# Attention's probabilities transposed by VectorE and through DRAM, the values scaled in place of them, and retention's output products among the filling

## The chip, the cores and the metric

One core of one Trainium2 chip runs the whole block. The metric is the device time in microseconds (us); lower is better. The kernel before takes 691.04 us, the median of three runs (690.86 to 691.95). Its engines are named as in the profile: PE is TensorE (matmuls, and transposes done as matmuls), PEld its weight loads, DVE is VectorE, ACT ScalarE, POOL GpSimd and SP SyncE, which issues nearly all DMA transfers. PSUM is the memory that matmuls write, in banks of 128 partitions x 512 float32; tiles are 128 partitions high.

## What is computed

A decoder block on 512 tokens of 1024 features, all in float32: retention (4 heads) and forgetting attention (8 heads of 64) beside each other, mixed by sigmoid gates, then an output product and a SwiGLU. The change touches the attention, the two output products and the gates. Cut to these:

```python
z = rmsnorm(x, g_mix) @ w_in              # q_r,k_r,v_r,g_r, q_f,k_f,v_f,f_f, a_r,a_f
o_r = silu(g_r) * groupnorm(retention(rotary(q_r), rotary(k_r), v_r))
y_r = o_r @ w_ret_o                        # 512 -> 1024
# forgetting attention, per head; c is the running sum of log sigmoid(f_f + b)
s = (q @ k.T) / 8 + c[:, None] - c[None, :]
s = where(key <= query, s, -inf)
p = softmax(s, axis=-1)                    # exp(s - max) divided by its row's sum
o_f = p @ v
y_f = o_f @ w_fox_o                        # 512 -> 1024
merged = sigmoid(a_r) * y_r + sigmoid(a_f) * y_f
x = x + merged @ w_out
x = x + swiglu(rmsnorm(x))
```

## The kernel before

Most products are made of three matmuls (`three`, L171): each float32 operand is split into a part that the fast matmul format holds exactly (`wh`, `xh`, cast by ScalarE in line 153 for weights) and the rest (`wl`, `xl`, subtracted by VectorE in line 154). A unit of weights is a tile `raw` of 128 x 1024 (512 KB), loaded by SyncE in line 146; each `split_w` (L157) splits the unit that was loaded ahead and asks for a later one.

TensorE's order is pinned: `in_order` (L65) ties every matmul to the one before it. The other engines' orders come from a scheduler, with a few ties made by `after`. The program walks through its stages with `fill(us)` between the steps: `Fill` (L283) is a queue of generators of independent matmuls, the filling, and takes that many microseconds' worth from its head; `fill.until(n)` empties it until n generators are left. The filling is the projections of queries, keys and values, then the gates' projections: `gates(mp)` (L755) makes two gates (g = 0 for retention, 1 for attention) of two feature tiles each, 48 matmuls of 512 columns for each g, whose results VectorE takes from PSUM times `r1` into `sg` (L759).

The attention is the loop of lines 847 to 862, a chain of 32 steps s: a pair of heads a (0 to 3), a head e of the pair, a query tile i from 3 down to 0, with (i + 1) x 128 keys that are not masked. A step has these parts:

- `fox_scores` (L692): two matmuls into a bank `sc` (two banks, `sc`); VectorE's `tensor_tensor_reduce` (L710) subtracts the scores from the bias tile `cb` and keeps the row minimum; ScalarE's exponential (L712) makes the probabilities `pr` and their row sums; VectorE takes the reciprocal (L713) and multiplies `pr` by it (L714).
- `fox_turn` (L717), three steps later (`LAG`): i + 1 transposes of 128 x 128 on TensorE (through `turn`, L75) into a bank `tp`, copied into the head's `pT` by VectorE for i = 3 (L727) and by ScalarE for the other tiles (L729): 80 transposes and 32 copies in all.
- `fox_values` (L731), once a pair: 8 float32 matmuls of `vf` by `pT` into one bank `sc`, split into `ofh` (ScalarE, L177) and `ofl` (VectorE, L178).
- `fox_prep` (L673), in four of a pair's eight steps: the scaled queries `tq` and keys `tk` with their low parts (VectorE, L689); of the keys, a DMA copies the half `tk` to the other partitions (L687). `fox_bias` (L645) fetches `cb`, a head's row spread over 128 partitions (L648, 256 KB).

Between the steps stand 0.63 to 1.57 us of filling (`SF`), before a pair's values 1.8 (`VF`). Lines 870 to 887 come next: for each pair of feature tiles the output products of retention (from `orh`, `orl`) and of attention (from `ofh`, `ofl`), 24 matmuls each, the sigmoids on ScalarE and four operations of VectorE for each tile. With the pinning off there, the scheduler places some of retention's products beside the attention's last steps. `merged @ w_out` follows (L939), then the SwiGLU.

An operation that the change takes over is already there for the heads of queries and keys: `turn_heads` (L653) transposes all 32 x 32 squares of a tile at once on VectorE (`STREAM_TRANSPOSE`), and `put_heads` (L660) puts the squares to DRAM and fetches them into their places.

## Time and profile before

| what | us |
|---|---|
| median of the three runs | 691.04 |
| the profiled execution, its own time | 690.54 |
| its span in the trace, first to last instruction | 688.5 |
| first score matmul to the start of the first attention output product | 182.93 to 262.26 |
| first values of the four pairs (start) | 204.56, 224.22, 243.63, 256.64 |
| first matmul of `merged @ w_out` | 311.2 |

All times of the trace count from the span's start. A row of the timeline has the start in us, the duration in us, engine, line, operation, result and operands, then in brackets how long the engine had been idle and what released it. Matmuls overlap: one of 512 columns is shown with 0.39 us, and the next one starts 0.23 us after it. A group's row has the busy sum in us and the mean of one in ns behind the first bar, and the idle time ahead of the group behind the second. A stretch's row has its length and then, for TensorE, weight loads, VectorE, ScalarE and GpSimd, the busy time in it with the number of instructions; then the granted clock, the DMA engines' share and GB/s. A row of DMA issues ends with the KB of one and the median us from issue to landing.

### The profile page before, as it was taken

Reading aid. Unit: us, or ns where it says so; the run is one execution under the profiler, and the core shown is the slowest. Engines: PE = TensorE matmul, PEld = TensorE weight load, DVE = VectorE, ACT = ScalarE, POOL = GpSimd, SP = SyncE. Lnnn points to the kernel's source line nnn. Section 1 sums busy time; section 2 is a strip of 40 time slices with the busy share of each in tenths; the row PEclk is TensorE's granted clock in tenths of the full one; section 3 lists DMA queues with packets and bytes.
Section 4 is the critical chain, followed back from the end, with each engine's and each line's share of the span. In section 5 each row is a group of like instructions: output and inputs, shape, how many; then the busy total and the mean of one; then the engine's idle time right before and its main releaser. Section 6 shows DMA issues by size and latency. Waiting matters only on the chain.

```text
span 688.5 us, 9502 instructions
## 1 busy us (share of the span) xinstructions
PE 682.9 (99%) x3487; PEld 572.6 (83%) x3487; DVE 538.0 (78%) x873; ACT 360.3 (52%) x542; POOL 70.2 (10%) x88
## 2 busy tenths in 40 slices
PE   9999999999999999999999999999999999999998
PEld 6888988888878778888888888888888898888997
DVE  6899478766598866647979998989999888557694
ACT  6767362332466666325566655565647475433341
POOL 0004941200132110000130000000000000000000
PEclk9999999999999999999999999999999999999999
DMA  8900314465432412238510615546362541642211
GB/s 285 419 34 32 124 62 137 109 181 136 160 107 78 137 47 78 93 99 298 214 61 1 243 33 144 152 117 180 89 178 60 131 145 32 187 149 66 105 75 62
DMA packets 85326, 86.73 MB, mean 126 GB/s; under 512 B 63000, under 2 KB 63640, under 8 KB 84768
## 3 DMA queue, kind: packets, MB, share of 16 engines
q1 hardware_dynamic: 85136, 86.12, 40.2%
q8 instruction: 27, 0.44, 0.3%
q14 instruction: 19, 0.16, 0.1%
q10 hardware_dynamic: 144, 0.02, 0.0%
HBM read 75.61 MB, written 4.21 MB: 116 GB/s over the span
## 4 chain that ended last, share of the span: by engine, by line
PE 91%; DVE 4%; DMA 2%; ACT 1%; issue 1%; SPq 1%; POOL 0%; ACTq 0%; DVEq 0%; POOLq 0%
PE acc L72 69%; PE sc L72 16%; PE tp L72 5%; PE tp L75 2%; DVE pr L710 1%; DMA raw<-in_w_dn_dram 1%; DMA raw<-in_w_tok_dram 0%; ACT pr L712 0%; DMA cb<-cd 0%; DVE ps L970 0%; DVE wl L154 0%; DVE pT L727 0%; SPq L1074 0%; ACT ps L969 0%; DVE pr L714 0%
## 5 line engine op out<-in xcount | busy, mean ns | idle before, releaser
L72 PE MATMUL acc<-ps,xfh 128*128 128x512 f32 (+1 forms) x576 | 166.6, 372 | 0.3 <-ACT us L1091 0.3
L72 PEld LDWEIGHTS acc<-ps,xfh 128*128 128x128 f32 x576 | 105.2, 188 | 19.2 <-ACT us L1091 0.5
L969 ACT CAST ps<-b 128x1024 fp32r<-128x1024 f32 (+1 forms) x84 | 82.3, 980 | 62.4 <-DVE b L978 27.4
L970 DVE TENSOR_TENSOR ps<-b,ps 128x1024 fp32r<-128x1024 f32 (+1 forms) x84 | 94.3, 1135 | 19.4 <-ACT ps L969 18.3
L72 PE MATMUL acc<-ps,xfl 128*128 128x512 f32 (+1 forms) x288 | 106.9, 371 | 0.0
L153 ACT CAST wh<-raw 128x1024 fp32r<-128x1024 f32 (+1 forms) x44 | 46.0, 1049 | 85.0 <-PE acc L72 60.2
L154 DVE TENSOR_TENSOR wl<-raw,wh 128x1024 fp32r<-128x1024 f32 (+1 forms) x44 | 56.5, 1287 | 18.5 <-ACT wh L153 18.4
L72 PEld LDWEIGHTS acc<-ps,xfl 128*128 128x128 f32 x288 | 54.3, 188 | 9.4
L72 PE MATMUL acc<-xh,wh 128*128 128x512 f32 x128 | 52.9, 413 | 0.0
L978 DVE TENSOR_TENSOR b<-b,b 128x1024 f32<-128x1024 f32 (+1 forms) x48 | 52.2, 1126 | 0.2 <-DMA b<-in_w_gu_dram 0.2
L72 PE MATMUL acc<-wh,xh 128*128 128x512 f32 (+2 forms) x144 | 50.4, 350 | 0.0
L72 PE MATMUL acc<-xh,wl 128*128 128x512 f32 x128 | 50.1, 392 | 0.0
L72 PE MATMUL acc<-xl,wh 128*128 128x512 f32 x128 | 50.0, 391 | 0.0
L72 PE MATMUL acc<-wh,xl 128*128 128x512 f32 (+2 forms) x144 | 49.4, 343 | 0.0
L72 PE MATMUL acc<-wl,xh 128*128 128x512 f32 (+2 forms) x144 | 49.3, 342 | 0.0
L72 PE MATMUL acc<-hl,ps 128*128 128x512 f32 x168 | 40.4, 389 | 0.0
L72 PEld LDWEIGHTS acc<-hl,ps 128*128 128x128 f32 x168 | 31.5, 188 | 6.6
L1091 ACT COPY us<-acc 128x512 f32<-128x512 f32 (+1 forms) x48 | 26.1, 550 | 15.6 <-PE acc L72 14.5
L72 PEld LDWEIGHTS acc<-wh,xh 128*128 128x128 f32 x144 | 27.2, 189 | 3.6 <-ACT wh L153 0.2
L72 PEld LDWEIGHTS acc<-wh,xl 128*128 128x128 f32 x144 | 27.2, 189 | 3.2
L1010 DVE TENSOR_TENSOR ps<-raw,ps 128x1024 fp32r<-128x1024 f32 x14 | 17.1, 1223 | 16.3 <-ACT ps L1007 16.3
L72 PEld LDWEIGHTS acc<-wl,xh 128*128 128x128 f32 x144 | 27.2, 189 | 3.0
(294 smaller groups left out, 1473.1 us busy)
## 6 DMA issues: line engine op xcount, KB each, us to landing
b<-in_w_gu_dram SPq DMA_DIRECT2D x40, 512.0 KB, 4.9
raw<-in_w_a_dram SPq DMA_DIRECT2D x16, 512.0 KB, 3.6
raw<-in_w_dn_dram SPq DMA_DIRECT2D x14, 512.0 KB, 4.8
pf<-squares SPq DMA_DIRECT2D x160, 32.0 KB, 1.9
blk<-in_w_vg_dram SPq DMA_DIRECT2D x8, 512.0 KB, 13.0
raw<-in_w_tok_dram SPq DMA_DIRECT2D x8, 512.0 KB, 3.4
raw<-in_w_y_dram SPq DMA_DIRECT2D x8, 512.0 KB, 3.7
raw<-in_w_o_dram SPq DMA_DIRECT2D x8, 512.0 KB, 3.8
```

Of the source, the lines that this page charges most:

```text
L72: in_order(nc.tensor.matmul(o, **kw))
L75: in_order(nc.tensor.transpose(out=o, in_=src, identity=ident))
L153: split_raw.last = (nc.scalar.copy(out=h[:, :width], in_=raw[:, :width]), tt(out=l[:, :width], in0=raw[:, :width], in1=f32(h)[:, :width], ...
L154: tt(out=l[:, :width], in0=raw[:, :width], in1=f32(h)[:, :width], op=ALU.subtract))
L710: nc.vector.tensor_tensor_reduce(out=pr[:, :n], in0=cb[:, :n], in1=sc[:, :n], scale=-1.0, scalar=3e38, op0=ALU.add, op1=ALU.min, accum_out=nm)
L969: part.cast = nc.scalar.copy(out=h, in_=raw)
L970: low = tt(out=l, in0=raw, in1=f32(h), op=ALU.subtract)
L978: queue(tt(out=raws[g][b][v], in0=raws[g][b][v], in1=raws[g][c][v], op=ALU.add))
L1010: tt(out=l, in0=raw, in1=f32(h), op=ALU.subtract)
L1091: copy = nc.scalar.copy(out=u_(tp, slot), in_=os[tp][:, :w])
```

## The change

The probabilities stay unnormalised: the reciprocal and the multiplication of each step go (L713, L714). The row sums of a pair's eight tiles are collected in `rs`, VectorE takes their reciprocals at once, and the result goes to DRAM (`rd`) and comes back spread over the partitions (`rw`). VectorE multiplies the values by `rw` in PSUM before they are split.

TensorE's transposes and their copies go too. `fox_turn` has VectorE transpose a tile's probabilities within 32 x 32 squares into the head's `psq` (1 or 2 instructions a tile: 32 of 256 elements a partition and 16 of 128 in all); `fox_put` puts `psq` to DRAM (640 KB a head), and `fox_get` fetches it with four DMAs of 160 KB into `pT`, which puts the squares into their places. The values are taken two pairs of steps after their scores began (in steps 16, 24, 32 and 40; the loop has nine trailing steps), and their columns stand by square.

The transfers of SyncE now keep the program's order (`move`), those of weights, bias tiles, keys and probabilities among them; a load of weights is asked for two `three`s after a unit was taken, in place of at once. Scores and values take turns over the four banks `sc` and `tp`. `gates(3)` stands in the filling whole, and behind it retention's four output products, each with its sigmoid and its multiplication; the last stage keeps the attention's output products. There are 16 tiles `sg` for 14, three `cb` for two.

```diff
+    def move(to, src):
+        ins = nc.sync.dma_start(out=to, in_=src)
+        if moves[0]:
+            if moves[1] is not None:
+                after(ins, moves[1])
+            moves[1] = ins
+        return ins
...
-    RAW, WB, SG, PT, CBUF = 2, 3, 14, 2, 2
-    RF, CF, PF, SF, LAG = (5.72, 4.64, 5.6, 4.6, 11.2), (3.0, 2.0, 2.26, 4.0), 5.9, (0.63, 0.83, 1.57, 1.4), 3
-    VF = 1.8
+    RAW, WB, SG, PT, CBUF, LEAD = 2, 3, 16, 2, 3, 2
+    RF, CF, PF, SF, LAG = (5.72, 4.64, 5.6, 4.6, 11.2), (3.0, 2.0, 2.26, 4.0), 5.9, (0.63, 0.83, 1.57, 1.4), 2
+    VF, TAIL = 1.8, 2.6
...
         h = fwk.tile([P, S], F32R, name=("tk", "tq")[part], tag=f"{('tk', 'tq')[part]}{e}", bufs=1)
         act(out=h[r], in_=zr, func=AF.Copy, scale=gr)
-        if part == 0:
-            nc.sync.dma_start(out=f32(h)[o], in_=f32(h)[r])
...
+    def next_bank():
+        fox["banks"] = fox.get("banks", 0) + 1
+        return bank(("sc", "tp")[fox["banks"] % 2])
...
-        sc = bank("sc")
+        sc = next_bank()
         mm(sc[:, :m], lhsT=tq[:, qs], rhs=tk[:, :m], start=True, stop=False)
         mm(sc[:, :m], lhsT=tq[:, qs], rhs=kl[:, :m], start=False, stop=True)
         pr = fwk.tile([P, n], F32, name="pr", tag=f"pr{i}", bufs=1)
         nm = sm.tile([P, 1], F32, name="nm", tag="nm", bufs=4)
-        rs = sm.tile([P, 1], F32, name="rs", tag="rs", bufs=4)
-        ri = sm.tile([P, 1], F32, name="ri", tag="ri", bufs=4)
         nc.vector.tensor_tensor_reduce(out=pr[:, :n], in0=cb[:, :n], in1=sc[:, :n], scale=-1.0, scalar=3e38,
                                        op0=ALU.add, op1=ALU.min, accum_out=nm)
-        fox["last"] = act(out=pr[:, :n], in_=pr[:, :n], func=AF.Exp, scale=-1.0, bias=nm, accum_out=rs)
-        nc.vector.reciprocal(out=ri, in_=rs)
-        ts(out=pr[:, :n], in0=pr[:, :n], scalar1=ri, scalar2=None, op0=ALU.mult)
+        fox["last"] = act(out=pr[:, :n], in_=pr[:, :n], func=AF.Exp, scale=-1.0, bias=nm, accum_out=fox["rs", a][:, e, i:i + 1])
         fox["pr", a, e, i] = pr
     def fox_turn(a, e, i):
-        pr, pT = fox["pr", a, e, i], fox["pT", a, e]
-        pt = bank("tp")
-        for j in range(i + 1):
-            turn(pt[:, j * P:(j + 1) * P], pr[:, j * P:(j + 1) * P])
-        row = pT[:, i * P:(i + 1) * P]
-        dst = bass.AP(tensor=row.tensor, offset=row.offset, ap=[row.ap[0], [384, i + 1], [1, P]])
-        src = pt[:, :(i + 1) * P].rearrange("p (j q) -> p j q", j=i + 1)
-        if i == 3:
-            nc.vector.tensor_copy(out=dst, in_=src)
-        else:
-            nc.scalar.copy(out=dst, in_=src)
+        if i == NT - 1:
+            fox["sq", a, e] = fwk.tile([P, 4, 10, 32], F32, name="psq", tag="psq", bufs=PSQ)
+        pr, to = fox["pr", a, e, i], fox["sq", a, e].rearrange("p b c j -> p c b j")
+        squares_ = pr.rearrange("p (k b j) -> p k b j", b=4, j=32)
+        for k0, k1, step in ((0, min(i, 1), 3), (2, i, 1)):
+            if k1 >= k0:
+                c = TRI[k0] + i
+                nc.vector.transpose(out=to[:, c:c + (k1 - k0) * step + 1:step], in_=squares_[:, k0:k1 + 1])
+    def fox_put(a, e):
+        pd = fox["pd", e] = drp.tile([4, 32, 4, 320], F32, name="pd", tag=f"pd{e}")
+        move(pd.rearrange("g m b x -> (g m) (b x)"), fox["sq", a, e].rearrange("p b c j -> p (b c j)"))
+        if e:
+            ri = sm.tile([P, 2, NT], F32, name="ri", tag="ri", bufs=2)
+            nc.vector.reciprocal(out=ri, in_=fox["rs", a])
+            rd = fox["rd", e] = drp.tile([2, NT, P], F32, name="rd", tag="rd")
+            move(rd.rearrange("e i p -> p e i"), ri)
+    def fox_get(a, e):
+        pT = fox["pT", a, e] = fwk.tile([P, 4, 320], F32, name="pT", tag="pT", bufs=PT)
+        for b in range(4):
+            move(pT[32 * b:32 * b + 32], fox["pd", e][:, :, b, :].rearrange("g m x -> m g x"))
+        if e:
+            rw = fox["rw", a] = fwk.tile([P, S], F32, name="rw", tag="rw", bufs=1)
+            for h, rows in enumerate((ra, rb)):
+                move(rw[rows], fox["rd", e][h:h + 1].rearrange("o i p -> o (i p)").broadcast_to([FD, S]))
     def fox_values(a):
-        av = bank("sc")
-        for j in range(NT):
+        av = next_bank()
+        o = av.rearrange("p (g i j) -> p g i j", g=4, i=NT)
+        for k in range(NT):
+            c = TRI[k] + k
             for e in range(2):
-                mm(av[e * FD:(e + 1) * FD, j * P:], lhsT=vf[:, j, (2 * a + e) * FD:(2 * a + e + 1) * FD],
-                   rhs=fox["pT", a, e][:, j * 512:j * 384 + 512], start=j == 0, stop=j == NT - 1)
-        split_ps(av, ofh[:, a, :], ofl[:, a, :])
+                mm(o[e * FD:(e + 1) * FD, :, k:, :].rearrange("p g i j -> p g (i j)"), lhsT=vf[:, k, (2 * a + e) * FD:(2 * a + e + 1) * FD],
+                   rhs=fox["pT", a, e][:, :, 32 * c:32 * (c + NT - k)], start=k == 0, stop=k == NT - 1)
+        o = o.rearrange("p g i j -> p i g j")
+        first = tt(out=o, in0=o, in1=fox["rw", a].rearrange("p (i g j) -> p i g j", i=NT, g=4), op=ALU.mult)
+        after(first, split_raw.last[1])
+        if a == 3:
+            after(first, y_ret.last)
+        h, l = (f[:, a, :].rearrange("p (i g j) -> p i g j", i=NT, g=4) for f in (ofh, ofl))
+        cast = nc.scalar.copy(out=h, in_=o)
+        after(cast, split_raw.last[0])
+        if a == 3:
+            after(cast, sigmoid.last)
+        tt(out=l, in0=o, in1=f32(h), op=ALU.subtract)
...
+    def y_ret(mp):
+        def evac(m2, acc):
+            s0 = sig[0, 2 * mp + m2]
+            sigmoid(s0)
+            y_ret.last = tt(out=s0, in0=acc, in1=s0, op=ALU.mult)
+        yield from feat(lambda u: w_y[0, mp], 1, orh, orl, evac)
...
-                tok_group(unit(1), evac_kf), tok_group(unit(0), evac_to(vf, AF.Copy)), gates(0), gates(1), gates(2), gates(3, (0,)))
+                tok_group(unit(1), evac_kf), tok_group(unit(0), evac_to(vf, AF.Copy)), gates(0), gates(1), gates(2), gates(3), *(y_ret(mp) for mp in range(4)))
...
     chain = [(a, e, i) for a in range(4) for e in range(2) for i in reversed(range(NT))]
-    for s in range(len(chain) + LAG + 2):
-        if s < len(chain) and s % 8 < 2:
-            fox_prep(s // 8, 1, s % 8)
-        if s % 8 in (4, 5) and s // 8 < 3:
-            fox_prep(s // 8 + 1, 0, s % 8 - 4)
+    for s in range(len(chain) + 9):
+        a, n = s // 8, s % 8
+        if n < 2 and a < 4:
+            fox_prep(a, 1, n)
+        if n in (4, 5) and a < 3:
+            fox_prep(a + 1, 0, n - 4)
         if s < len(chain):
             fox_scores(*chain[s])
-        v = s - LAG - 1
-        if v >= 0 and v % 8 == 7:
-            fill(VF + 2.0 * (v == len(chain) - 1))
-            if v == 7:
-                fill.until(4)
-            fox_values(v // 8)
+        if n == 1 and a < 4:
+            fox_twice(1)
+        if n == 5 and a < 3:
+            fox_twice(0)
+        if n in (1, 5) and 2 * a + n // 4 + 2 < FH:
+            fox["bias"].append(fox_bias(2 * a + n // 4 + 2))
+        if n == 0 and a > 1:
+            fill(VF)
+            if a == 2:
+                fill.until(8)
+            if a == 5:
+                ready.append(split_raw(begun.pop(0)))
+            fox_values(a - 2)
+        if n == 7 and a < 4 or n == 3 and 0 < a < 5:
+            fox_put(*chain[s - 7 + 3][:2])
+        if n in (1, 5) and 0 < a < 5:
+            fox_get(*chain[s - 9 + 3][:2])
         if LAG <= s < len(chain) + LAG:
             fox_turn(*chain[s - LAG])
-        fill(SF[chain[s][2]] if s < len(chain) else SF[0] + 0.8)
-    fill.until(3)
...
+    fill.until(0)
     for mp in range(4):
-        if mp > 0:
-            fill.until(3 - mp)
-            if mp == 3:
-                run(gates(mp, (1,)))
         ys = []
-        for g, (yh, yl) in enumerate(((orh, orl), (ofh, ofl))):
-            run(feat(lambda u: w_y[g, mp], 1, yh, yl, lambda m2, acc: ys.append(acc)))
+        run(feat(lambda u: w_y[1, mp], 1, ofh, ofl, lambda m2, acc: ys.append(acc)))
         for m2 in range(2):
             m = 2 * mp + m2
             s0, s1 = sig[0, m], sig[1, m]
-            for sg in (s0, s1):
-                after(act(out=sg, in_=sg, func=AF.Sigmoid), fox["last"])
-            tt(out=s0, in0=ys[m2], in1=s0, op=ALU.mult)
-            tt(out=s1, in0=ys[2 + m2], in1=s1, op=ALU.mult)
+            sigmoid(s1)
+            tt(out=s1, in0=ys[m2], in1=s1, op=ALU.mult)
```

Of the names below, `acc` tiles are the filling's PSUM banks, `wl` a weight unit's low part, `sg` a gate, `pr` a tile of probabilities, `nm` its row minimum; line numbers are those of the kernel that the rows are from.

VectorE before, just ahead of the first score step (its last row): the low part `wl_1821` belongs to the weight unit that the filling takes up six matmuls ahead of the first scores, the two others to later units.

```order
L759 TENSOR_TENSOR sg_1741<-acc_1618,r1_89 128x512
L154 TENSOR_TENSOR wl_1821<-raw_1818,wh_1820 128x1024
L154 TENSOR_TENSOR wl_1917<-raw_1914,wh_1916 128x1024
L759 TENSOR_TENSOR sg_1809<-acc_1743,r1_89 128x512
L759 TENSOR_TENSOR sg_1814<-acc_1744,r1_89 128x512
L154 TENSOR_TENSOR wl_2053<-raw_2050,wh_2052 128x1024
L710 ISA pr_1843,nm_1844<-cb_1836,sc_1840 128x512
```

VectorE after, the same place: that unit's low part is `wl_1827`, and `tq`, `kl` are low parts of queries and keys (L700).

```order
L807 TENSOR_TENSOR sg_1745<-acc_1622,r1_89 128x512
L700 SCALAR_TENSOR_TENSOR tq_1766<-qf_647,gq_88,tq_1766 64x512
L700 SCALAR_TENSOR_TENSOR tq_1858<-qf_647,gq_88,tq_1858 64x512
L700 SCALAR_TENSOR_TENSOR kl_1738<-kf_648,ce_84,tk_1763 64x512
L700 SCALAR_TENSOR_TENSOR kl_1739<-kf_648,ce_84,tk_1840 64x512
L807 TENSOR_TENSOR sg_1817<-acc_1747,r1_89 128x512
L165 TENSOR_TENSOR wl_1827<-raw_1756,wh_1826 128x1024
L807 TENSOR_TENSOR sg_1822<-acc_1748,r1_89 128x512
L730 ISA pr_1848,nm_1849<-cb_1761,tp_1845 128x512
```

The low part stood ahead of the two gate copies of the unit before it; now it stands between them, behind `sg_1817`. The low parts of the two later units have gone from this place.

VectorE before, at the low part of the first pair's values (`ofl_1831`): the copy of `pT` and the scalings of L714 stand among the steps.

```order
L154 TENSOR_TENSOR wl_2358<-raw_2355,wh_2357 128x1024
L727 COPY pT_2030<-tp_2137 128x4x128
L178 TENSOR_TENSOR ofl_1831<-sc_2126,ofh_1830 128x512
L710 ISA pr_2163,nm_2164<-cb_2156,sc_2160 128x512
L710 ISA nm_2164 128x1
L713 RECIPROCAL ri_2166<-rs_2165 128x1
L714 TENSOR_SCALAR pr_2163<-pr_2163,ri_2166 128x512
L710 ISA pr_2192,nm_2193<-cb_2156,sc_2189 128x384
```

VectorE after, around the scaling of the first pair's values in their bank (`sc_2185`) and their low part (`ofl_1839`):

```order
L744 STREAM_TRANSPOSE psq_2139<-pr_2107 128x4x32
L744 STREAM_TRANSPOSE psq_2139<-pr_2135 128x2x4x32
L744 STREAM_TRANSPOSE psq_2139<-pr_2152 128x4x32
L730 ISA pr_2168,nm_2169<-cb_2028,tp_2165 128x512
L730 ISA nm_2169 128x1
L807 TENSOR_TENSOR sg_2178<-acc_2002,r1_89 128x512
L807 TENSOR_TENSOR sg_2183<-acc_2003,r1_89 128x512
L776 TENSOR_TENSOR sc_2185<-sc_2185,rw_2119 128x4x4x32
L785 TENSOR_TENSOR ofl_1839<-sc_2185,ofh_1838 128x512
```

The scaling and the low part stand behind all transposes of the second pair's second head (`psq_2139`) and behind the first reduction of the third pair; before, 12 steps had been reduced at that place, and now 17.

SyncE before, at the time of the first pair: bias tiles, halves of keys and weights.

```order
L648 DMA cb_2028<-cd_1726 128x512
L687 DMA tk_1923<-tk_1923 64x512
L146 DMA raw_2355<-in_w_a_dram 128x1024
L687 DMA tk_2024<-tk_2024 64x512
L648 DMA cb_2156<-cd_1726 128x512
```

SyncE after, the first pair's trip: a put `pd` for each head, its fetches `pT`, and the row sums' `rd` and `rw`.

```order
L73 DMA pd_1980<-psq_1886 128x1280
L73 DMA raw_2011<-in_w_a_dram 128x1024
L73 DMA tk_1989<-tk_1989 64x512
L73 DMA cb_2028<-cd_1730 128x512
L73 DMA pT_2030<-pd_1980 32x4x320 x4
L73 DMA pd_2067<-psq_1961 128x1280
L73 DMA rd_2071<-ri_2069 128x8x1
L73 DMA tk_2078<-tk_2078 64x512
L73 DMA cb_2112<-cd_1730 128x512
L73 DMA pT_2114<-pd_2067 32x4x320 x4
L73 DMA rw_2119<-rd_2071 64x512 x2
L73 DMA raw_2123<-in_w_a_dram 128x1024
```

In each head's stretch of the queue, one put and four fetches have come in, and a weight load follows behind the fetches.

46 lines of the change are left out of this document (32 added, 14 removed).

## The prediction

> **What bounds the kernel now.** The first view read is the page: totals, then the chain that ended last.
>
> ```profile
> span 688.5 us, 9502 instructions
> PE 682.9 (99%) x3487; PEld 572.6 (83%) x3487; DVE 538.0 (78%) x873; ACT 360.3 (52%) x542; POOL 70.2 (10%) x88
> PEclk9999999999999999999999999999999999999999
> PE 91%; DVE 4%; DMA 2%; ACT 1%; issue 1%; SPq 1%; POOL 0%; ACTq 0%; DVEq 0%; POOLq 0%
> ```
>
> TensorE is busy for 682.9 of 688.5 us at the full granted clock, and the chain runs through it for 91% of the span. So a matmul taken away is worth its place in TensorE's queue, as long as nothing new makes TensorE wait. The second view is the table of stretches around the attention: the attention steps up to 262 us, then the output products.
>
> ```profile
> 200.00:240.00 40.00, 39.33 (x211) 30.40 (x210) 33.83 (x91) 24.94 (x60) 10.80 (x18) 1.00 0.35 103
> 262.00:305.00 43.00, 43.00 (x191) 35.61 (x190) 26.13 (x34) 15.66 (x21) 0.00 (x0) 1.00 0.30 95
> 305.00:345.00 40.00, 40.00 (x179) 33.11 (x178) 32.94 (x42) 20.68 (x29) 4.43 (x3) 1.00 0.65 227
> ```
>
> The numbers behind each stretch are TensorE, weight loads, VectorE, ScalarE and GpSimd. In the attention VectorE has 33.83 of 40 us: it is the next bound. TensorE's only wait named there is for it, 0.5 us in the list of waits:
>
> ```profile
> PE sc L72 <- DVE nm L710: 0.5, 2, 0.4
> ```
>
> **The change, part by part.** *The 80 transposes leave TensorE.* Their own busy time is no price, since matmuls are pipelined; the price is the distance between starts. The timeline shows the end of one score step without and one with four transposes, and the group of all 80:
>
> ```profile
> 186.58 0.28 PE L72 MATMUL sc<-kl,tq 128*128 128x256 f32 x1
> 186.70 0.40 PE L72 MATMUL acc<-xh,wh 128*128 128x512 f32 x1
> 186.93 0.40 PE L72 MATMUL acc<-xl,wh 128*128 128x512 f32 x1
> ...
> 188.20 0.29 PE L72 MATMUL sc<-kl,tq 128*128 128x256 f32 x1
> 188.32 0.60 PE L75 MATMUL tp<-ctab,pr 128*128 128x128 f32 x4
> 188.68 0.48 PE L72 MATMUL acc<-xh,wh 128*128 128x512 f32 x1
> 188.99 0.40 PE L72 MATMUL acc<-xl,wh 128*128 128x512 f32 x1
> L75 PE MATMUL tp<-ctab,pr 128*128 128x128 f32 x80 | 14.0, 275 | 0.1
> ```
>
> From the score to the second filling matmul it is 0.35 us without and 0.79 with them: 0.44 for four, 0.11 each, 80 x 0.11 = 8.8 us. The filling, the scores and the value products keep their matmuls and column counts; the order of their blocks in the value products (runs of 32 columns instead of one run) I take at nothing; no row shows such runs, and one contiguous pair's value products last 2.3 us (below), so 0 to 2 us a pair are the ends. With four banks for scores instead of two the 0.5 us of waits for VectorE in line 710 go as well: -9.3 in all.
>
> *VectorE.* It loses the rows of this group view, and gains transposes, whose only price in before is that of 512 elements:
>
> ```profile
> L727 DVE COPY pT<-tp 128x512 f32<-128x512 f32 x8 | 5.5, 683 | 0.7 <-PE tp L75 0.7
> L713 DVE RECIPROCAL ri<-rs 128x1 f32<-128x1 f32 x32 | 5.1, 158 | 6.4 <-ACT pr L712 6.2
> L714 DVE TENSOR_SCALAR pr<-pr,ri 128x512 f32<-128x512 f32 x8 | 5.0, 621 | 0.2
> L714 DVE TENSOR_SCALAR pr<-pr,ri 128x384 f32<-128x384 f32 x8 | 3.8, 473 | 0.2
> L714 DVE TENSOR_SCALAR pr<-pr,ri 128x256 f32<-128x256 f32 x8 | 2.8, 351 | 0.2
> L714 DVE TENSOR_SCALAR pr<-pr,ri 128x128 f32<-128x128 f32 x8 | 2.3, 284 | 0.2
> L710 DVE CUSTOM_DVE_ANT_0 pr<-cb,sc 128x512 f32<-128x512 f32 x8 | 5.4, 678 | 0.0
> L710 DVE CUSTOM_DVE_ANT_0 pr<-cb,sc 128x256 f32<-128x256 f32 x8 | 3.3, 408 | 0.0
> L1063 DVE STREAM_TRANSPOSE squares<-us x20: 668/703/706, 399.2 to 583.2; 128x512 f32<-128x512 f32 x20
> ```
>
> Removed: 5.5 + 5.1 + 13.9 = 24.5 us. Added: 32 transposes of 256 elements and 16 of 128. The reductions of line 710 fall by 0.27 us from 512 to 256 elements; so I take 0.43 and 0.30 (ends: half and a quarter of 0.70, and 0.70 whatever the size): 18.6 us, with four scalings in PSUM at 0.69 (as the low parts of line 178) and four reciprocals 22 us. VectorE's load hardly falls while TensorE's path gets 9 us shorter. How near they come is read from the value products, which start at
>
> ```profile
> 204.56 0.65 PE L72 MATMUL sc<-pT,vf 128*64 128x512 f32 x2 [0.15 <-DVE nm L710]
> 206.87 0.66 PE L75 MATMUL tp<-ctab,pr 128*128 128x128 f32 x4
> ...
> 224.22 0.65 PE L72 MATMUL sc<-pT,vf 128*64 128x512 f32 x2
> ...
> 243.63 0.65 PE L72 MATMUL sc<-pT,vf 128*64 128x512 f32 x2
> ```
>
> A pair of heads takes TensorE 243.63 - 224.22 = 19.4 us, and 17.2 without its 20 transposes. VectorE has 33.83/40 of 19.4 = 16.4 us a pair now, 6.1 less and 5.5 more after: 15.8 of 17.2. That fits on the mean. Its order (shown with the change) is lumpy: by the first value products it has worked off 16 score steps, where before it was 12. From the first reduction to the low part of the first values stand 17 reductions, 24 transposes, 8 low parts of queries and keys, 4 of weights, 4 gate copies and four small ones: some 33.6 us of durations, less about 0.07 for each of 61 (back to back they start that much earlier than durations say), plus 1 to 3 us of waiting for exponentials: 31 to 33 us after the first scores. By the spacings above TensorE wants the bank of these values again 33.8 us after them. So it is close: 0 to 2 us lost at the first pair, the same at the second, none at the third, which has no more queries and keys beside it.
>
> *The transfers.* Each head is put (640 KB) and fetched (four of 160 KB), all in SyncE's fixed order; a fetch waits there until the put has landed. The nearest rows (KB each, us to landing):
>
> ```profile
> raw<-in_w_a_dram SPq DMA_DIRECT2D x16, 512.0 KB, 3.6
> zd<-zsq SPq DMA_DIRECT2D x8, 256.0 KB, 5.0
> cb<-cd SPq DMA_DIRECT2D x8, 256.0 KB, 3.8
> qf<-zd SPq DMA_DIRECT2D x4, 256.0 KB, 5.3
> tk<-tk SPq DMA_DIRECT2D x8, 128.0 KB, 2.4
> ```
>
> I take 4.2 for the put (between the weights' 3.6 and the 5.0 of small pieces), and for four fetches 1.2 of issue and 2.4 to 3.8: 8 to 9.5 us. The tightest is the second head's: VectorE has its last square about 17.5 us after the first scores, and the values come 26 us after: 0 to 1 us late. A wait here gives VectorE the same time to catch up, so the two are one term: **+1.2 us, 0 to 5**. Behind a waiting fetch stand one weight load and the next put; that weight unit is used some 10 us later, so it is covered. The keys' doubling copy of the next pair is in the same queue and lands about 1 us ahead of its use. The last pair has 105 filling matmuls (24 us) before its values and 33 more behind, so its trip and the scaling, cast and low part are hidden.
>
> *One late weight part.* Before the chain the order puts the low part of the weight unit that begins six matmuls ahead of the first scores behind a gate copy that waits for TensorE; before, it stood in front:
>
> ```profile
> 174.16 1.23 DVE L154 TENSOR_TENSOR wl<-raw,wh 128x1024 fp32r<-128x1024 f32 x1 [1.73 <-ACT wh L153]
> 181.09 1.37 DVE L759 TENSOR_TENSOR sg<-acc,r 128x512 f32<-128x512 f32 x2 [2.68 <-PE acc L72]
> 182.02 0.39 PE L72 MATMUL acc<-xh,wl 128*128 128x512 f32 x1
> ```
>
> The gate copy can't start before 181.09 and takes half of 1.37; the low part then ends at 181.75 + 1.23 = 182.98, and the matmul that started at 182.02 needs it, plus its weight load: **+1.1 us**. If the copy moved aside it would be 0.
>
> *Retention's output in the filling* moves 96 matmuls and eight multiplications, adds none, and leaves the later stage with half its VectorE work per output pair; the stretch from 262 to 345 us has no idle TensorE now and VectorE at 26.13 of 43 and 32.94 of 40. The first gate and up weights are split up to 10 us later than now, inside that stretch; I take 0 (end: +1). The divisions by row sums and the rest of the moved loads cost nothing on the path.
>
> Sum: -8.8 - 0.5 + 1.2 + 1.1 = -7.0 us. The profiled execution took 690.54 us, its span and 2.0 around it, which gives 683.5; the median of the runs, 691.04, lies 0.5 above it: **684.0 us**.
>
> **The rivals.** *All is hidden* (chance 0.14): the two new terms vanish, -9.3, 681.7 us. For it: both are differences of about 1 us between estimates. Against it: the order of the late weight part is fixed.
>
> *VectorE becomes the bound* (0.14): a transpose of 256 or 128 elements costs 0.70 as one of 512. Up to the first values that is 16 x 0.27 + 8 x 0.40 = 7.5 us more, about 6 of it beyond what TensorE leaves, and 1 more in each of the next pairs: -8.2 + 8 = -0.2, 690.8. Against it: line 710 falls with the size.
>
> *The trip through DRAM is late* (0.10), the slower one. The query heads' turn in before is such a trip, with pieces of 128 bytes:
>
> ```profile
> 111.33 3.23 SPq L665 DMA_DIRECT2D zd<-zsq  x4
> 117.21 6.12 SPq L668 DMA_DIRECT2D qf<-zd  x4
> ```
>
> From the first put to the last fetch's landing it is 12.0 + 5.3 = 17.3 us. At that price the first values come 9 us late, and two heads a pair hold SyncE's queue for 24 us against TensorE's 17.2, 6.8 more for each of two further pairs: +22.6 - 8.2 = +14, 705 us. It decides once a head holds the queue for over 8.6 us. Against it: the pieces are 5120 and 1280 bytes here, as in rows of 3.6 and 3.8 us. The Trainium skill, "VectorE: DVE Perf Modes", section "Rules for kernel authors", speaks for this rival: it sends a 128x128 transpose to TensorE where a PSUM destination will do, and VectorE's only for 32x32 blocks. Its section "The three transpose paths" gives 390 ns for TensorE's; this trace has 0.11 us from start to start, so leaving TensorE is worth less than by the page.
>
> **How the numbers follow.** The forecast has 0.62, its own range 682 to 687 (the joint term from 0 to 4). 0.2% of 691 is 1.4 us, about what a measurement can tell from no change. The range 681.5 to 688.8 leaves out the late trip and most of the VectorE case, and takes in the joint term to its end of 5 (687.8) and the ends of the filling. Faster by over 0.2%: forecast, all hidden and a share of the VectorE case, 0.83; within: 0.06; slower: 0.11.
>
> **What would show it.** Right: no transposes of probabilities on TensorE, the span from the first scores to the last values' end shorter by 5 to 9 us against the same filling, one wait of about 1 us for a low part just before the first scores, and waits of at most 2 us each for the fetched probabilities or a bank at the first two value products. Wrong: TensorE waiting over 3 us for the fetch at each pair, transposes of 256 elements at 0.7, or new idle time after 262 us.

## The result and the profile after

The changed kernel takes 713.13 us, the median of four runs (712.57 to 714.69), against 691.12 for the kernel before: a ratio of 1.032, 95% interval 1.030 to 1.0339. The forecast was 684.0 and its range ended at 688.8. The direction was wrong.

The page of the changed kernel: span, busy times, granted clock and the chain that ended last.

```profile
span 710.8 us, 9375 instructions
...
PE 689.8 (97%) x3407; PEld 568.8 (80%) x3407; DVE 534.4 (75%) x857; ACT 352.9 (50%) x518; POOL 70.1 (10%) x88
...
PEclk9999999999998998999999999999999999999999
...
PE 85%; DMA 9%; DVE 3%; issue 1%; SPq 1%; ACT 1%; DVEq 0%; ACTq 0%
```

VectorE isn't the bound: its busy time is about what it was (534.4 us for 538.0) in a longer span. What is new is 9% of the chain in DMA, and two places in which the granted clock dips. TensorE's list of waits names the transfers:

```profile
PE tp L83 <- DMA tk<-tk: 6.8, 1, 6.8
PE tp L83 <- DMA pT<-pd: 4.1, 1, 4.1
PE sc L83 <- DMA tk<-tk: 3.1, 1, 3.1
...
PE acc L83 <- DVE wl L165: 0.8, 1, 0.8
```

The largest wait isn't for the fetched probabilities but for `tk<-tk`, the doubling of a head's keys, a transfer that the kernel before has too. SyncE's queue around it, start and length of issue:

```profile
205.10 0.34 SPq L73 DMA_DIRECT2D pd<-psq  x1
207.28 0.38 SPq L73 DMA_DIRECT2D rd<-ri  x1
207.76 0.54 SPq L73 DMA_DIRECT2D tk<-tk  x1
208.39 0.54 SPq L73 DMA_DIRECT2D cb<-cd  x1
210.25 3.69 SPq L73 DMA_DIRECT2D pT<-pd  x4
217.90 1.11 SPq L73 DMA_DIRECT2D rw<-rd  x2
```

The keys' half was issued in time, at 207.76, ten microseconds ahead of its use. Just ahead of it stands `rd<-ri`, the reciprocal row sums: 4 KB, written to DRAM as 1024 pieces of 4 bytes. The median times to landing between 180 and 300 us (KB each, then us):

```profile
pd<-psq SPq DMA_DIRECT2D x8, 640.0 KB, 6.7
pT<-pd SPq DMA_DIRECT2D x32, 160.0 KB, 4.2
...
cb<-cd SPq DMA_DIRECT2D x6, 256.0 KB, 8.4
...
tk<-tk SPq DMA_DIRECT2D x7, 128.0 KB, 7.3
rd<-ri SPq DMA_DIRECT2D x4, 4.0 KB, 11.9
```

The smallest transfer takes longest, and `tk` and `cb` went to 7.3 and 8.4 us from 2.5 and 3.4 in the same stretch of the kernel before. TensorE at that place, and the same place in stretches of 4 us (after the busy times: granted clock, DMA share, GB/s):

```profile
211.13 0.28 PE L83 MATMUL sc<-kl,tq 128*128 128x256 f32 x1
218.25 0.77 PE L83 MATMUL tp<-tk,tq 128*128 128x512 f32 x1 [6.83 <-DMA tk<-tk]
218.81 0.63 PE L83 MATMUL tp<-kl,tq 128*128 128x512 f32 x1
219.24 0.63 PE L83 MATMUL acc<-xh,wh 128*128 128x512 f32 x1
219.67 0.63 PE L83 MATMUL acc<-xl,wh 128*128 128x512 f32 x1
```

```profile
210.00:214.00 4.00, 1.42 (x8) 0.99 (x6) 2.94 (x9) 1.91 (x5) 0.92 (x2) 1.00 0.98 13
214.00:218.00 4.00, 0.00 (x0) 0.00 (x0) 3.52 (x9) 1.33 (x4) 0.00 (x0) 0.74 0.45 9
218.00:222.00 4.00, 3.75 (x9) 3.04 (x10) 0.70 (x2) 0.81 (x2) 0.87 (x2) 0.50 0.91 198
222.00:226.00 4.00, 3.71 (x17) 1.70 (x16) 1.38 (x2) 0.00 (x0) 0.00 (x0) 0.91 1.05 330
```

From 210 to 214 us the times of the DMA packets add up to 0.98 of the 16 engines' time, and they move 13 GB/s. And the stall is paid twice: behind it the granted clock is 0.50, and the matmuls of 512 columns start 0.43 us apart in place of 0.23 until about 223 us. The Trainium skill, "TensorE: Matmul & The Clock Gate", Part 1, has the array's clock at half rate after an idle window of about 3.4 us. The 6.83 us here fit that; but in this trace the clock is also 0.50 from 244 to 246 us, behind the wait of only 3.09 us, so here a shorter wait was enough.

The larger stretches that answer to those of before. VectorE has less to do in the first of them, since TensorE stands still there:

```profile
200.00:240.00 40.00, 31.68 (x137) 24.26 (x136) 27.84 (x74) 18.83 (x45) 8.31 (x15) 0.91 0.83 185
262.00:305.00 43.00, 38.87 (x164) 28.26 (x163) 17.65 (x27) 15.07 (x21) 0.00 (x0) 0.92 0.64 164
```

The stalls don't hold all of it. Three stretches of TensorE's order, cut at the first score matmul and at the first matmul of `merged @ w_out`, give where the 22.3 us of the two spans came from:

| stretch | before | after | difference |
|---|---|---|---|
| to the first scores | 182.93 | 187.27 | +4.3 |
| first scores to `merged @ w_out` | 128.29 | 143.31 | +15.0 |
| from there to the end | 377.3 | 380.2 | +2.9 |

The first and the last stretch run code that the change hardly touches. Some 1.6 us of the first are waits that the kernel before doesn't have: 0.75 for the late weight part, 0.8 for parts of weights at the very start. Most of the rest is a slower beat. The 96 matmuls of attention's output products, the first and the last of them, in the changed kernel:

```profile
308.19 0.39 PE L83 MATMUL acc<-ofh,wh 128*128 128x512 f32 x1
...
330.35 0.40 PE L83 MATMUL acc<-ofh,wl 128*128 128x512 f32 x1
```

That is 22.16 us for 95 distances, 0.2333 us each. In the kernel before, matmuls of this size stand 0.2267 us apart where nothing disturbs them, here 2.9% more, with a granted clock of 1.00 in both. In the product that follows, from the first `mgh` matmul on, it is 0.2267 again. What is different about the slower operands is where they lie: the change keeps row sums in other small tiles (two buffers each of `rs` and `ri` for four), which makes the pool at the upper end 128 bytes smaller and moves everything on that side up: `xh` from byte 194,048 of a partition, a multiple of 512, to 194,176. `mgh` lies on the other side.

So two theories stood to be tested: **small pieces** (`rd` holds up what is issued behind it) and **address** (an operand off its boundary slows each matmul). Their rivals: the late trip of the prediction (the probabilities' own 640 KB are too slow), and a clock that was lower by chance.

### The profile page after: what moved, and what is told of

It reads as the page before. It is cut to its first block, busy times and chain, and to the rows that moved or that the text cites. A ratio compares the mean times of both kernels' runs of the same rounds, so it can differ in the third digit from the quotient of the medians.

```text
span 710.8 us, 9375 instructions
## 1 busy us (share of the span) xinstructions
PE 689.8 (97%) x3407; PEld 568.8 (80%) x3407; DVE 534.4 (75%) x857; ACT 352.9 (50%) x518; POOL 70.1 (10%) x88
## 4 chain that ended last, share of the span: by engine, by line
PE 85%; DMA 9%; DVE 3%; issue 1%; SPq 1%; ACT 1%; DVEq 0%; ACTq 0%
PE acc L83 65%; PE sc L83 14%; PE tp L83 5%; DMA pd<-psq 4%; DMA pT<-pd 3%; DMA raw<-in_w_tok_dram 1%; SPq L73 1%; PE tp L86 1%; DMA raw<-in_w_a_dram 1%; DVE pr L730 0%; DVE wl L165 0%; ACT ps L1042 0%; DVE psq L744 0%; DVE ps L1043 0%; DVE b L1051 0%
## 5 line engine op out<-in xcount | busy, mean ns | idle before, releaser
L83 PEld LDWEIGHTS acc<-ps,xfh 128*128 128x128 f32 x576 | 105.1, 188 | 20.3 <-ACT us L1164 0.6
L83 PE MATMUL acc<-xh,wl 128*128 128x512 f32 x128 | 51.7, 404 | 0.8 <-DVE wl L165 0.8
L83 PE MATMUL acc<-xl,wh 128*128 128x512 f32 x128 | 51.7, 404 | 0.0
L732 ACT ACTIVATE pr<-pr,nm 128x512 f32<-128x512 f32 (+3 forms) x32 | 18.0, 561 | 25.8 <-DVE nm L730 25.6
L83 PEld LDWEIGHTS acc<-xh,wl 128*128 128x128 f32 x128 | 24.9, 194 | 7.1 <-DVE wl L165 1.2
```

Source lines behind the costliest of these rows:

```text
L83: in_order(nc.tensor.matmul(o, **kw))
L732: fox["last"] = act(out=pr[:, :n], in_=pr[:, :n], func=AF.Exp, scale=-1.0, bias=nm, accum_out=fox["rs", a][:, e, i:i + 1])
```

## The experiments

All are timed beside the kernel before on the same chip. Medians in us, and the ratio to before with its 95% interval:

| run | median | ratio |
|---|---|---|
| e1_align | 707.91 | 1.0237 (1.0220 to 1.0254) |
| e2_no_rd | 692.86 | 1.0023 (1.0012 to 1.0034) |
| e3_before_shift | 696.98 | 1.0081 (1.0066 to 1.0096) |
| e4_before_rd | 697.91 | 1.0092 (1.0077 to 1.0107) |
| e5_rows | 688.55 | 0.9963 (0.9943 to 0.9982) |
| e6_act_queue | 718.16 | 1.0389 (1.0373 to 1.0404) |
| e7_rows_low | 687.07 | 0.9940 (0.9925 to 0.9955) |
| e8_rows_late | 695.70 | 1.0066 (1.0048 to 1.0084) |
| e9_low_later | 683.84 | 0.9901 (0.9885 to 0.9916) |
| e10_half | 707.90 | 1.0247 (1.0231 to 1.0264) |
| e11_shift256 | 691.35 | 1.0004 (0.9994 to 1.0014) |
| e12_shift64 | 696.38 | 1.0076 (1.0061 to 1.0091) |
| e13_pieces32 | 685.87 | 0.9916 (0.9901 to 0.9931) |
| e14_column | 706.10 | 1.0202 (1.0156 to 1.0248) |
| e15_before_rd_scratch | 697.77 | 1.0083 (1.0066 to 1.0100) |

**The address.** In the changed kernel the padding is made larger, in the kernel before it is taken out or changed.

```diff
-    PAD_CST, PAD_FTOK, PAD_SM = 104, 104, 32
+    PAD_CST, PAD_FTOK, PAD_SM = 104, 104, 64
```

> The changed kernel with 128 bytes more of padding in the pool of small tiles, so that xh, xl, orh, orl, ofh and the FFN's operands lie where they lay before (xh at byte 194,048 of a partition, a multiple of 512, and not at 194,176). Address theory: the 2.9% slower spacing of the matmuls from 20 to 330 us (0.2333 for 0.2267 us) goes, and the time falls by 6 to 8 us to 705 to 707; the three stalls of the attention stay. Rival, that the chip's clock was a little lower in that execution: no change within 1 us, and the spacing stays 0.2333.

Measured: 707.91, 5.2 us less than the change. The same 96 matmuls in e1_align:

```profile
307.64 0.39 PE L83 MATMUL acc<-ofh,wh 128*128 128x512 f32 x1
...
329.17 0.39 PE L83 MATMUL acc<-ofh,wl 128*128 128x512 f32 x1
```

21.53 us for 95 distances, 0.2266 each. The beat is that of before; the gain is a little under the 6 to 8 us expected, since with it the waits grew (9.6, 5.3 and 4.1 us).

```diff
-    sm.tile([P, PAD_SM], F32, name="pad", tag="pad", bufs=1)
```

> The kernel before without its 128 bytes of padding in the pool of small tiles, so that xh, xl, orh, orl, ofh and the FFN's operands lie 128 bytes higher, as in the changed kernel; nothing else is different. Address theory: the spacing of matmuls up to 311 us goes from 0.2267 to 0.2333 and the time rises by 6 to 8 us to 697 to 699. Rival (clock by chance): within 1 us of 691.

Measured: 696.98, 5.8 us more than the kernel before, from an edit that takes away a tile which nothing reads. That is the lower end of what was expected. In its trace the first scores start at 185.26 (182.93 before) and the part behind the output products is 2.8 us longer, as in the changed kernel. Two more places of the same operands, with `PAD_SM` 96 and 16:

> The kernel before with xh, xl, orh, orl, ofh and the FFN's operands 256 bytes lower, at 256 modulo 512. If the rows of 512 float32 have to begin at a multiple of 512 bytes for the faster spacing: 696 to 698 as with 128 bytes. If a multiple of 256 is enough: 691.

> The kernel before with the same operands 64 bytes higher, at 64 modulo 512. If any start that is off the boundary costs the same part of each matmul: 696 to 698. If the cost goes with the distance from the boundary: 693 to 695. If a multiple of 64 is enough: 691.

Measured: 691.35 at 256 modulo 512, the interval around 1; 696.38 at 64. So 0 and 256 are as good as each other, and 64 and 128 cost the whole kernel about the same 5 to 6 us. Of the places tried, those at a multiple of 256 bytes are fast.

An operand that is streamed through the array isn't the only one that counts. In the first projections `xh` and `xl` are the other operand, the one that is loaded into the array as weights (the second name of a row), and the streamed `wh` and `wl` stay at 0. Two matmuls, 23 distances apart, in the kernel before and in e3_before_shift:

```profile
44.45 0.39 PE L72 MATMUL sc<-wh,xh 128*128 128x512 f32 x1
49.67 0.39 PE L72 MATMUL sc<-wl,xh 128*128 128x512 f32 x1
```

```profile
44.83 0.40 PE L72 MATMUL sc<-wh,xh 128*128 128x512 f32 x1
50.18 0.40 PE L72 MATMUL sc<-wl,xh 128*128 128x512 f32 x1
```

That is 0.2270 us each before and 0.2326 with `xh` and `xl` at 128; the same 23 distances take 0.2335 each at 64 (44.87 to 50.24 us in e12_shift64). Streamed, they do depend on the place: the last 48 output products stand 0.2266 us apart at 0, 0.2321 at 128, but 0.2287 at 64 (303.00 to 313.75 us for 47 distances).

**The small transfer.** First it is left out of the change:

```diff
-            rd = fox["rd", e] = drp.tile([2, NT, P], F32, name="rd", tag="rd")
-            move(rd.rearrange("e i p -> p e i"), ri)
...
-                move(rw[rows], fox["rd", e][h:h + 1].rearrange("o i p -> o (i p)").broadcast_to([FD, S]))
+                move(rw[rows], cd[h:h + 1, :].broadcast_to([FD, S]))
```

> The changed kernel without the transfer of the reciprocal row sums to DRAM (1024 pieces of 4 bytes a pair); rw is fetched from two rows of the bias instead, with the same bytes, so the values are scaled by other numbers. Theory of the small pieces: they hold the DMA engines for about 10 us a pair and the keys' halves and the fetches behind them; without them the stalls of 6.8 and 3.1 us and most of the 4.1 go, with the lowered clock behind each, and the time falls by 15 to 21 us to 692 to 698. Rival, that the puts and fetches of 640 KB a head are themselves too slow for SyncE's fixed order: under 5 us, 708 or more.

Measured: 692.86, 20.3 us less. TensorE's waits in the attention are now

```profile
PE tp L83 <- DMA pT<-pd: 1.1, 1, 1.1
PE acc L83 <- DVE wl L165: 0.8, 1, 0.8
PE sc L83 <- issue: 0.5, 1, 0.5
```

and none for keys. All puts and fetches of probabilities are still there, so the late trip falls as the main cause. (The fetch of `rw` no longer waits for the row sums either; e5_rows and e13_pieces32 below keep a put at this place.) The same from the other side, the small transfer alone put into the kernel before, with the address kept:

```diff
-        rs = sm.tile([P, 1], F32, name="rs", tag="rs", bufs=4)
+        if e == 0 and i == NT - 1:
+            fox["rs", a] = fwk.tile([P, 2 * NT], F32, name="rs", tag="rs", bufs=2)
+        rs = fox["rs", a][:, e * NT + i:e * NT + i + 1]
...
+        if s % 8 == 3 and s > 8:
+            rd = drp.tile([2 * NT, P], F32, name="rd", tag="rd")
+            nc.sync.dma_start(out=rd.rearrange("i p -> p i"), in_=fox["rs", s // 8 - 1])
```

> The kernel before with one transfer more for each pair: the row sums of its eight tiles to DRAM in the shape of the change (1024 pieces of 4 bytes), read by nobody. Theory of the small pieces: it takes near 10 us to land here too and what is issued behind it lands late (keys' halves at 8 to 12 us for 2.4); TensorE waits for a half at one or more pairs and the time rises by 3 to 12 us. Rival (the trip of the probabilities is what is slow): it lands in about 2 us and the time rises by under 1 us.

Measured: 697.91, 6.7 us more; from the first scores to `merged @ w_out` it takes 6.0 us longer (184.57 to 318.88). Landing times in its attention:

```profile
tk<-tk SPq DMA_DIRECT2D x6, 128.0 KB, 8.2
rd<-rs SPq DMA_DIRECT2D x3, 4.0 KB, 10.6
```

The keys' halves land at 8.2 us, against 2.5 without it, with no probabilities in the queue at all. What TensorE waited for was something else than expected, though: its longest wait there (2.26 us, with a granted clock of 0.56 from 218 to 220 us behind it) comes through VectorE and GpSimd from a bias tile `cb`, issued at 207.25 and 9.2 us on its way.

This trace also shows when the pieces move, since nothing else hides them. The second `rd` is issued at 222.31 us and lands 10.6 us later. All small packets lie ahead of 226 us; then the 16 engines move nothing (DMA share and GB/s are the last two numbers), although a weight load is issued at 228.51 and a keys' half at 228.93:

```profile
222.00:226.00 4.00, 4.00 (x21) 3.32 (x21) 2.85 (x7) 2.66 (x7) 0.24 (x1) 1.00 0.62 101
226.00:231.00 5.00, 4.88 (x24) 3.02 (x24) 3.99 (x13) 2.64 (x9) 2.65 (x4) 1.00 0.00 0
```

So it isn't, or not only, that moving the pieces keeps the engines busy. One part of the change that no run had touched, its smaller scratch for descriptors, was set in this kernel too:

> As e4_before_rd (the kernel before with the 1024 pieces of 4 bytes a pair, 697.9), with the changed kernel's smaller scratch for DMA descriptors (1024 for 16384 bytes a partition). If that scratch has a part in the late landings: 700 or more. Rival, that it has none: 697 to 699.

Measured: 697.77. It has no share.

**Which queue.** In e6_act_queue the put of `rd` is issued by ScalarE (`nc.scalar.dma_start`) in place of `move`.

> As the changed kernel with the address put right (707.9), but the 1024 pieces of 4 bytes are issued by ScalarE's queue and not by SyncE's. If what the pieces hold is SyncE's queue alone, the keys' halves behind them come through and the time falls to 688 to 690. If they hold the 16 DMA engines that all queues share, other transfers still land late: 698 to 708.

Measured: 718.16, above both. The time alone doesn't tell the two apart: SyncE's next transfer, the fetch of `rw`, waits for this put to land (up to 14.0 us), and with it all that is queued behind; TensorE waits 13.9 us for the probabilities. So a queue in fixed order hands on a late transfer of another queue. But the trace does, at the first pair: the put is issued at 205.93 us, and two of the fetches that SyncE issues from 207.14 on, which don't wait for it, land just as late (us from issue to landing last; 4.2 is the median in the changed kernel):

```profile
rd<-ri ACTq DMA_DIRECT2D x1, 4.0 KB, 11.6
```

```profile
pT<-pd SPq DMA_DIRECT2D x2, 160.0 KB, 12.3
```

The keys' half issued ahead of the put, at 205.17, lands after 2.2 us. So the pieces delay what another queue issues behind them too, and to move them there doesn't help.

**What of the transfer costs.** Half of the pieces, then the same bytes in pieces of 32, then one column (all with the address put right, against 707.91):

```diff
-            move(rd.rearrange("e i p -> p e i"), ri)
+            move(rd[0:1].rearrange("e i p -> p e i"), ri[:, 0:1, :])
```

That is e10_half; in e13_pieces32 the line is `move(rd, ri)` with `rd` of the shape [P, 2, NT], and in e14_column both sides are cut to one column, `rd[0:1, 0:1]` and `ri[:, 0:1, 0:1]`.

> As e1_align (the change with the address put right, 707.9), but of the reciprocals only those of the first head of a pair go to DRAM, 512 pieces of 4 bytes for 1024 (both halves of rw are fetched from them, so the second head is scaled by other numbers). If the time goes with the number of pieces, the transfer lands in about half of 12 to 13 us, and most of the stalls, which lie behind it, go: 690 to 699. If one such transfer costs what it costs whatever its pieces: 705 or more.

> As e1_align (707.9), but the reciprocals go to DRAM as they lie, 128 pieces of 32 bytes, and rw is fetched from two rows of the bias, so the values are scaled by other numbers. Theory that a transfer cut into single elements is what takes 11 to 13 us whether it has 512 or 1024 of them: 687 to 689, as with the eight rows. Rival, that any short transfer at this place, waiting for a row sum, costs it: 700 or more.

> As e13_pieces32, but only one tile's reciprocals go to DRAM, 128 pieces of 4 bytes that lie together there. If single elements cost the same whatever their number, as from 1024 to 512: 700 or more. If the number counts below 512, or pieces that lie together are taken as a row: 687 to 691.

Measured: 707.90, 685.87 and 706.10 (701.79 to 709.26). Landing times of the transfer in the three, in this order:

```profile
rd<-ri SPq DMA_DIRECT2D x4, 2.0 KB, 11.7
```

```profile
rd<-ri SPq DMA_DIRECT2D x4, 4.0 KB, 4.5
```

```profile
rd<-ri SPq DMA_DIRECT2D x4, 0.5 KB, 9.5
```

The guess that the number of pieces sets the time falls: 1024, 512 and 128 pieces of 4 bytes cost about the same, and 128 pieces of 32 bytes, eight times the bytes of e14_column in the same number, cost nothing that shows. It is the 4-byte pieces. The Trainium skill, "DMA: Bandwidth & Descriptors", section "Specifications", puts the bound for full rate at 512 bytes, with a read-modify-write below; here pieces of 32 bytes, well below it, already land in time. Why a piece of 4 bytes is so different, and why their number hardly counts, stays open. In all these runs neighbouring pieces also lie beside each other in DRAM; whether their size or that neighbourhood counts was not varied.

**The change with this put right.** The reciprocals are turned by one small TensorE transpose a pair into eight rows of 512 bytes:

```diff
+    def fox_rows(a):
+        few = next_bank()[0:2 * NT, 0:P]
+        turn(few, fox["ri", a].rearrange("p e i -> p (e i)"))
+        row = fwk.tile([2 * NT, P], F32, name="row", tag="row", bufs=1)
+        nc.scalar.copy(out=row, in_=few)
+        move(fox["rd", 1].rearrange("e i p -> (e i) p"), row)
```

> The whole change, correct, with the address of the first experiment put right and the reciprocals turned by one small TensorE transpose a pair into eight rows of 128, so that their way to DRAM has 8 pieces of 512 bytes for 1024 of 4. Theory of the small pieces with the address as the second cause: both losses go, 692.9 of the run without that transfer less the 5.2 of the address, 687 to 688.5. Rival, that any transfer at this place (it waits for a row sum in SyncE's fixed order) is the cost and not its pieces: the stalls on the keys' halves come back and it takes 695 or more.

Measured: 688.55, faster than before, 0.9963 (0.9943 to 0.9982). What still stood between it and the forecast were waits at the value products, at the late weight part (0.8 us) and for the row sums of the small transpose (2.0 us).

> As e5_rows, and the low part of the weight unit that begins six matmuls ahead of the first scores is put ahead of the two gate copies again, as before the change. By the prediction's step on the late weight part: TensorE's wait of 0.8 us there goes and the time falls by 0.8 us against e5_rows. Rival: the wait moves to the next low part or the first reduction, no change.

The edit splits that unit's weights ahead of the stretch and ties the gate copies behind its low part. Measured: 687.07; the intervals of the two ratios overlap, so the times don't settle it. In the trace the wait of 0.78 us ahead of the first scores is gone, and one of 1.5 for another low part stands at 206.7 us, near the place where e5_rows waited 2.0 for the row sums.

> As e5_rows, but the values of the first three pairs are taken two steps later (3.1 us of filling and scores more) with a third buffer for the fetched probabilities. If what is left of the joint term (about 4 us in three places at the value products) is the fetch landing late, it goes and the time falls by 2 to 4 us against e5_rows. If VectorE is what is late, the work merely comes later and the time stays within 1 us of e5_rows.

Measured: 695.70, 7 us more. The fetch theory is half right: each of the four value products now runs through in 2.30 to 2.31 us. But one of TensorE's waits has grown, from 1.3 us in e5_rows:

```profile
PE acc L83 <- DVE wl L165: 7.8, 8, 2.0
```

In SyncE's fixed order a weight load that stood ahead of the next head's fetch (issued at 212.34 us in e5_rows) now stands behind it (221.91 us), and that fetch waits for its put to land. So, on top of e7_rows_low, the values were moved by one step only, which leaves them ahead of the fetch:

```diff
-        if n == 0 and a > 1:
+        if n == 1 and 1 < a < 5 or n == 0 and a == 5:
```

> As e7_rows_low (687.1), with the values of the first three pairs taken one step later, but still ahead of the next fetch, and without a third buffer; in SyncE's fixed order no weight load moves behind a fetch that stood ahead of it by more than one place. Fetch theory: the 1.2 to 1.6 us that each of the first three value products lost go, 683 to 685. Rival, from the two steps later that lost 7 us: the weight loads come late again and TensorE waits for low parts, 687 or more.

Measured: 683.84 (683.66 to 685.54), ratio 0.9901 (0.9885 to 0.9916): the fastest of all. Its page, and a value product of it beside that of e5_rows (second and third fence), which stood still after two of its matmuls:

```profile
span 681.9 us, 9393 instructions
...
PE 673.2 (99%) x3411; PEld 563.7 (83%) x3411; DVE 534.2 (78%) x857; ACT 353.4 (52%) x522; POOL 71.6 (11%) x88
```

```profile
213.18 2.37 PE L83 MATMUL sc<-pT,vf 128*64 128x512 f32 x16
```

```profile
213.39 1.07 PE L83 MATMUL tp<-pT,vf 128*64 128x512 f32 x2
214.63 0.61 PE L83 MATMUL tp<-pT,vf 128*64 128x512 f32 x2 [0.16 <-issue]
```

From the first scores to `merged @ w_out` it takes 304.70 - 183.67 = 121.0 us, 7.3 less than before. With the stalls gone VectorE is nearer its limit than before the change, 36.07 us of 40 for 33.83, and low parts of weights are what TensorE still waits for (3.0 us in all):

```profile
200.00:240.00 40.00, 39.09 (x193) 29.75 (x192) 36.07 (x97) 24.24 (x59) 11.14 (x20) 1.00 0.88 264
```

## Why the prediction was wrong, point by point

- **The step that failed** is the last sentence of the part on retention's output: "The divisions by row sums and the rest of the moved loads cost nothing on the path." The division's way through DRAM is the 4-byte put. It cost 20.3 us (713.13 less 692.86), through waits for keys and probabilities that landed late and the lowered clock behind them. The prediction priced the put and fetch of the probabilities with care and passed over the smallest transfer of the change, whose shape, 128x8x1, stood in SyncE's order.
- **A cost that no step had**: 5.2 us of the address (713.13 less 707.91; 5.8 in the kernel before). The prediction looked at what the change does to each engine's queue and not at where it moves operands.
- Taken one by one they make 25.5 of the 29.1 us between forecast and result. They don't simply add up: with the address right the three long waits are longer (19.0 us for 14.0). With both gone at once (e13_pieces32, 685.87) it is 27.3 us, which leaves 1.9 to the other terms.
- **The joint term**, 1.2 us with ends at 0 and 5, was mis-sized. In e2_no_rd the first three value products took 2.98, 4.48 and 3.03 us for 2.31, and the scores beside them waited 0.17 and 0.49: 4.2 us in all, still within its ends. The trip through DRAM took longer than priced: in e5_rows the put took 4.9 us for the 4.2 assumed, the issue of four fetches 1.8 for 1.2, a fetch 4.1 for 2.4 to 3.8, and the waits at its second and third value product are put down to the fetch (0.46 and 1.54 us). With the values one or two steps later the products run through; how much of the lateness began with VectorE's squares wasn't measured apart.
- **The 80 transposes**: right. The first eight score steps take 13.80 us before (182.93 to 196.73) and 12.20 in e1_align (183.80 to 196.00), the filling the same; 1.6 us for 14 transposes is 0.11 each.
- **VectorE's transposes**, taken as 0.43 and 0.30: right, as the group of all 48 in the changed kernel shows (shortest, median and longest, in ns). With that the rival of a VectorE bound, whose condition was 0.70 for each, falls. Its load was priced well too: 15.8 of 17.2 us a pair is 0.92, and e9_low_later has 36.07 of 40, 0.90.

```profile
L744 DVE STREAM_TRANSPOSE psq<-pr x48: 269/402/447, 190.7 to 264.4; 128x256 f32<-128x256 f32 x32, 128x128 f32<-128x128 f32 x16
```

- **The value products' new column order**, taken as nothing: right, 2.30 to 2.31 us where they don't wait.
- **The late weight part**, 1.1: found at its place, at 0.75 us in the changed kernel.
- **Retention's output at no cost**: right; no wait of TensorE lies between the attention and `merged @ w_out` in e2_no_rd. In e9_low_later one of 1.5 us does, for a weight's low part (264.41 us).
- **The rival of the late trip** named 705 us and the slower side, and its signs, waits of over 3 us, came. But its mechanism, the size of the probabilities' pieces, wasn't the cause: with all of them in place and the 4-byte pieces gone the kernel is at 685.87.

The forecast of 684.0 is what the change makes once its two unpriced costs are gone, the late weight part is back in front and its values come a step later. That the numbers meet is luck in part and doesn't make the prediction right: the kernel as it was changed is 3.2% slower.

## What to carry to other kernels

Price each transfer by the size of its pieces before its bytes: a 4 KB put in single float32 took longer than 640 KB and delayed the transfers behind it, put alone into the kernel before as well. When a change alters the size of any pool, compare the addresses of the matmuls' operands, since 128 bytes cost 5 to 6 us here. And with a queue in fixed order, a shift of work is also a shift of loads past waits: look at what comes to stand behind a transfer that waits.

## What the runs showed of the hardware

- Matmuls of 512 columns start 0.2267 us apart with their operands at 0 or 256 bytes modulo 512, and 0.2321 to 0.2333 apart with the streamed operand at 128. With the operand that is loaded as weights off its place it is 0.2326 at 128 and 0.2335 at 64; with the streamed one at 64 it is 0.2287. Kernels with them at 64 and at 128 take 5 to 6 us longer than at 256.
- A DRAM write in 4-byte pieces landed after a median of 9.5 to 13.0 us in the changed kernel and its variants, with 128 pieces as with 1024, and transfers issued behind it landed late, on another queue too (12.3 us for a usual 4.2); in pieces of 32 bytes it took 4.5 us. In e4_before_rd the engines moved nothing from 226 to 231 us while such a write and two later transfers were on their way.
- A stall of 6.8 us was followed by some 4 us at a granted clock of 0.50, so that it cost about a third more than it lasted; waits of 3.09 us (changed kernel) and 2.26 us (e4_before_rd) were followed by a lowered clock too.
